# D weights copied by DMA into small float32r tiles and transposed from there

## Chip, cores and metric

The kernel runs on one core of one Trainium2 chip. The metric is the device time of one execution in microseconds (us), as the median of several runs. The names of the engines in the profile: PE is TensorE (matmuls, and transposes, which are matmuls with an identity), DVE is VectorE, ACT is ScalarE, POOL is GpSimd, SP is SyncE, which issues nearly all DMA transfers.

## What is computed

Two layers of a transformer encoder over 2048 tokens of width 1024. Each layer has an RMS norm, an input projection whose columns feed four groups of attention heads (A dense, B sliding window, C two-dimensional neighbourhood, D differential), a gate on every branch, an output projection and a residual add. The change touches group D, whose weights are a difference of two softmaxes:

```
def body(qi):                      # one block of 128 queries
    sc = einsum('bqkgcd,bskcd->cbkgqs', qi, k) * scale
    p = softmax(sc, axis=-1)       # c = 0, 1
    w = p[0] - lam * p[1]
    return einsum('bkgqs,bskd->bqkgd', w, v)
```

There are two key/value heads (kv), two query heads for each (g), and two halves c.

## The kernel before

**Stages of a layer.** First the D columns of the input projection are computed for all 16 token tiles. Then comes the *D stretch*: 32 D units (2 kv times 16 query tiles t), with the remaining projections (groups A, B and C) as *filler*. Then the pools of that part are closed (`switch`) and the units of A, B and C follow. The output projection ends the layer.

**A D unit.** `d_scores` loads the queries and the gate and makes, for each g and each c, four score matmuls S of 128x512 (line 496). VectorE copies each out of PSUM with its row maximum (line 497). After four of them a small step on VectorE (line 503, with the junk tile jk) makes the negative maximum, and ScalarE takes the exponential of the 128x2048 row in place (line 504). When both c of a g are done, `comb` (line 723) forms w on VectorE in the tile P, which holds both g: 128 x 2 x 2048 float32. Then `dense_front` runs in 8 slots: in each, four 128x128 float32 transposes go to one PSUM tile PTp (line 513), and one copy on ScalarE (line 474) puts the result back over the 256 columns of P that were read. After the eighth slot `dense_back` makes the outputs: O (line 520), 32 matmul instructions, and `fin_d` normalises, gates and stores.

**The order.** `drive` interleaves slots: while unit k is transposed, the scores of unit k + 1 are made, and `fillers` advances the projections by 12.2 steps a slot. The projection matmuls are called z (lines 320, 322, 324: three for each of 8 weight tiles). A scheduler then fixes the order on each engine at build time. It may move instructions of the D stretch forward and back, z above all. At run time every engine works its list strictly in order, SyncE too: a transfer whose wait is not met holds everything behind it on SyncE. In the A, B and C part the order on TensorE is that in which the code is written.

**Two ways to transpose.** `transpose_raw` (line 94) takes a float32r source and views PSUM as float32r. The other way, `PE.transpose` with `idn`, takes float32. `dense_front` uses the second.

**Other tiles of the change.** `gt` holds the gate of a unit, `st2` the staging tiles of the weights of the projections (wst) on their way from memory, 128 KB each.

```
for h in range(2):
    for a in range(2):
        j = i * 2 + a
        PE.transpose(tp[:, (h * 2 + a) * 128:(h * 2 + a + 1) * 128], p[:, h, j * 128:(j + 1) * 128], idn)
evac(p[:, :, c], tp.rearrange("p (h k) -> p h k", h=2), i in u["ev"])
```

Of the kernel before, what the change touches and what calls it, by code (L numbers as in the profile page):

```python
# [12 lines left out]
F32 = mybir.dt.float32  # L13
F32R = mybir.dt.float32r
# [9 lines left out]
NT = S // 128  # L24
# [3 lines left out]
GAP2 = 2  # L28
# [45 lines left out]
def trunk_kernel(ctx, tc, x, norm_g, w_in, w_out, qn_a, kn_a, sink_b, rpb_c, lam_q1, lam_k1, lam_q2, lam_k2,  # L74
                 subln_d, final_g, rope, bmask, out, depth=DEPTH):
    nc = tc.nc
# [15 lines left out]
    def transpose_raw(dst, src):  # L92

        PE.transpose(dst.bitcast(F32R), src, idr)
# [164 lines left out]
    for l in range(depth):  # L259
# [93 lines left out]
        with tc.tile_pool(name="wd", bufs=16, reuse_waits="tile") as wp, tc.tile_pool(name="st", bufs=3, reuse_waits="tile") as st:  # L353
# [13 lines left out]
            p1 = ExitStack()  # L367
# [71 lines left out]
            for t in range(NT):  # L439
                h = hs.pop(t)  # L440
# [21 lines left out]
        with tc.tile_pool(name="sm", bufs=6, reuse_waits="tile") as sm, \  # L462
# [7 lines left out]
            def evac(dst, src, on_v):  # L470
                if on_v:
                    V.tensor_copy(dst, src)
                else:
                    A.copy(dst, src)  # L474
# [4 lines left out]
            def tick():  # L479
                for e in list(later):  # L480
                    e[0] -= 1
                    if e[0] <= 0:
                        later.remove(e)
                        e[1]()
# [5 lines left out]
            def dense_scores(q_list, k_ap, scale, nscale, zacc, p):  # L490
                mx = sm.tile([128, 4], F32, tag="mx", name="mx")
                for j in range(4):
                    s = sps.tile([128, 512], F32, tag="s", name="S")
                    c = j * 512
                    for i, q in enumerate(q_list):
                        PE.matmul(s, lhsT=q, rhs=k_ap[:, c:c + 512], start=(i == 0), stop=(i == len(q_list) - 1))  # L496
                    V.tensor_scalar(p[:, c:c + 512], s, 1.0, None, op0=ALU.mult, op1=ALU.max, accum_out=mx[:, j:j + 1])  # L497
                    tick()
                    if j < 3:
                        yield  # L500
                nm = sm.tile([128, 1], F32, tag="nm", name="nm")
                jk = sm.tile([128, 4], F32, tag="jk", name="jk")
                V.tensor_scalar(jk, mx, nscale, None, op0=ALU.mult, op1=ALU.min, accum_out=nm)  # L503
                A.activation(p, p, ACTF.Exp, bias=nm, scale=scale, accum_out=zacc)  # L504


            def dense_front(u, i):
                p, c = u["p"], slice(i * 256, (i + 1) * 256)
                tp = next(tpool).tile([128, 512], F32, tag="t", name="PTp")
                for h in range(2):  # L510
                    for a in range(2):
                        j = i * 2 + a
                        PE.transpose(tp[:, (h * 2 + a) * 128:(h * 2 + a + 1) * 128], p[:, h, j * 128:(j + 1) * 128], idn)  # L513
                evac(p[:, :, c], tp.rearrange("p (h k) -> p h k", h=2), i in u["ev"])
# [91 lines left out]
                return rz  # L606

            def load_gate(g, t, i):
                gt = ov.tile([128, 128], F32, tag="gt", name="gt", bufs=7)
                if g == "C":  # L610
                    rg, ch = divmod(t, 2)
                    src = bass.AP(tensor=gc_d.tensor, offset=gc_d.offset + (256 * rg + 32 * ch) * 256 + i * 128,
                                  ap=[[16384, 4], [256, 32], [1, 128]])
                    nc.sync.dma_start(out=gt, in_=src)
                else:
                    nc.sync.dma_start(out=gt, in_=(gd_d[t] if g == "D" else gs_d[g, t])[:, i, :])
                return gt
# [108 lines left out]

            if True:
                ph2 = ExitStack()
                st = ph2.enter_context(tc.tile_pool(name="st2", bufs=5, reuse_waits="tile"))
                wp = ph2.enter_context(tc.tile_pool(name="w2", bufs=10, reuse_waits="tile"))  # L730
                zp = ph2.enter_context(tc.tile_pool(name="z2", bufs=2, reuse_waits="tile"))
                zps = ph2.enter_context(tc.tile_pool(name="zps2", bufs=2, space=PSUM, reuse_waits="tile"))
# [129 lines left out]
                def filler():  # L862
                    need = []
                    for c, tiles in plan:
                        need += [(c, t) for t in tiles]
                    last_use = {}
                    resident = {t: ht[l, t] for t in range(HALF)}
                    pend = pend_all
                    group = {}
                    for i, (c, tiles) in enumerate(plan):  # L870
                        group[i] = tiles
                    wcur = wpre + [load_w(wp, st, k, plan[0][0][1], 256) for k in range(len(wpre), KD)]
                    for i, ((grp, c0, post), tiles) in enumerate(plan):
                        nxt = plan[i + 1] if i + 1 < len(plan) else None
                        wnext = []
                        if i == 6:
                            build_rep(l, zp.tile([128, 256], F32, tag="qs", name="rbuf", bufs=3))
                        for n, t in enumerate(tiles):
                            lastt = n == len(tiles) - 1
                            if t not in resident:  # L880
                                h = big.tile([128, 2, D], F32R, tag="b", name="ht2")
                                nc.sync.dma_start(out=h.bitcast(F32), in_=ht_d[l, t])
                                resident[t] = h
                            h = resident[t]
                            z = zps.tile([128, 256], F32, tag="z", name="z")
                            for k in range(KD):
                                for _ in in_proj_k(z, h, wcur[k], k):
                                    yield
                                if k == KQ and len(pend) > 1:
                                    pend.pop(0)()  # L890
                                if k == 2 and i >= KA0:
                                    next(side, None)
                                if lastt and nxt and len(wnext) < KD:
                                    wnext.append(load_w(wp, st, len(wnext), nxt[0][1], 256))
                                yield
                            pend.append(post(grp, t, z) or (lambda: None))
                            if nxt and t not in nxt[1]:
                                resident.pop(t)
                                m = nxt[1][n] if len(nxt[1]) == len(tiles) else None
                                if m is not None and m not in resident:  # L900
                                    h = big.tile([128, 2, D], F32R, tag="b", name="ht2")
                                    nc.sync.dma_start(out=h.bitcast(F32), in_=ht_d[l, m])
                                    resident[m] = h
                            progress[0] += 1
                        wcur = wnext

                progress = [0]
                fill = filler()
                p1p = ph2.enter_context(tc.tile_pool(name="p1", bufs=1, reuse_waits="tile"))
                if True:  # L910
                    kds = {(0, 0): kd0[0], (0, 1): kd0[1]}

                    def get_kd(kv):
                        def f(c):
                            if (kv, c) not in kds:
                                k_ = big2.tile([128, S], F32R, tag="b", name="kdt")
                                nc.sync.dma_start(out=k_.bitcast(F32), in_=kd_d[0][:, c, :])
                                kds[kv, c] = k_
                            return kds[kv, c]
                        return f  # L920
                    units = [dict(kv=kv, t=t, k=get_kd(kv), qp=dv, s=d_scores, par=True, ns=16, nv=8, ev=(), fin=fin_d, fb=6 + kv,
                                  p1=p1p, fixed=False, gap=GAP2, front=dense_front, back=dense_back, get_o=own_o,
                                  v=lambda h, j, kv=kv: vd[:, j, kv * 64:(kv + 1) * 64]) for kv in range(2) for t in range(NT)]

                    for u in units:
                        u["fp"] = lambda: tps.tile([128, 512], F32, tag="t", name="fin")
                    for u in units[-2:]:
                        u["f1"], u["f2"] = 3, 5
                    units_d = [[u] for u in units]
# [64 lines left out]
            def b_scores(u):  # L994
                kv, t = u["kv"], u["t"]
                qh, qlo = u["q"]()
                u["g"] = load_gate("B", t, kv)
                j0, j1 = max(t - 1, 0), min(t + 2, NT)
                n = (j1 - j0) * 128
# [223 lines left out]
```

## Time and profile before

| | us |
|---|---|
| median of 3 runs | 3578.99 (3578.23 to 3581.57) |
| the profiled execution | 3577.38 |
| its span | 3575.6 |
| D stretch, layer 0: first S to last S | 184.2 to 1066.6 |
| D stretch, layer 1 | 1953.7 to 2834.6 |
| first S of group A | 1073.9 and 2841.8 |
| first matmul of the output projection | 1623 and 3390 |

The mean granted clock of TensorE is 0.99 of full speed. A row of a group names a line, an engine, an operation, the tiles (out<-in), shapes and a count, then the busy time, the mean duration in ns and the idle time ahead with what ended it. A row of a timeline begins with start and duration in us. Matmuls overlap each other, so their cost is read from the distance between starts. A row of windows begins with the stretch and its length, then busy us (and count) of PE, its weight loads PEld, DVE, ACT and POOL, then the granted clock, the busy share of the DMA engines and GB/s.

### The profile page before, as it was taken

How to read it: one execution, taken by the hardware profiler on the slowest of the kernel's cores; microseconds unless marked ns; L12 is line 12 of the kernel's file. 1: busy time of each engine (PE TensorE's matmuls, PEld its weight loads, DVE VectorE, ACT ScalarE, POOL GpSimd, SP SyncE). 2: the span in 40 equal slices, each digit the busy share in tenths (PEclk: the TensorE clock that was granted, in tenths of full speed). 3: DMA queues.
4: the chain of work that ended last, by engine and by line, in shares of the span. 5: the costliest groups of instructions: out<-in, count | busy, mean ns of one | idle time of the engine just before them, and what ended most of it. 6: DMA issues, size and time to landing. Idle time of an engine off the chain costs nothing.

```text
span 3575.6 us, 71573 instructions
## 1 busy us (share of the span) xinstructions
PE 3434.2 (96%) x25232; PEld 2961.5 (83%) x25232; DVE 2494.0 (70%) x7827; ACT 2110.5 (59%) x3963; POOL 955.3 (27%) x1604
## 2 busy tenths in 40 slices
PE   7999999999989999999999999999999899899999
PEld 7989889898967777887899898988889577688787
DVE  4377877778877887773233878787777788777733
ACT  4455656556667777771043556665566678777711
POOL 3455333553200001001034553256331000000000
PEclk9999999999999999999999999999999999999999
DMA  4532234333232345335435323253231332543243
GB/s 136 195 108 86 75 93 150 103 85 87 70 95 76 92 106 138 92 102 178 141 125 187 98 79 91 76 179 90 82 83 60 99 87 82 138 114 97 88 160 112
DMA packets 355777, 387.47 MB, mean 108 GB/s; under 512 B 59802, under 2 KB 298586, under 8 KB 350298
## 3 DMA queue, kind: packets, MB, share of 16 engines
q1 hardware_dynamic: 351098, 367.17, 34.7%
q10 hardware_dynamic: 4320, 15.73, 1.3%
q8 instruction: 199, 3.26, 0.4%
q14 instruction: 160, 1.31, 0.1%
HBM read 258.83 MB, written 123.91 MB: 107 GB/s over the span
## 4 chain that ended last, share of the span: by engine, by line
PE 78%; DVE 10%; DMA 3%; ACT 3%; POOL 2%; issue 2%; SPq 0%; DVEq 0%; ACTq 0%; POOLq 0%
PE O L520 11%; PE S L496 10%; PE y L218 10%; PE PTp L513 10%; PE z L320 10%; PE z L324 9%; PE z L322 9%; DVE P L497 4%; PE Obc L539 2%; PE PTp L531 2%; DVE P L723 2%; ACT P L504 2%; PE Sc L1043 1%; DVE wt L314 1%; DMA wst<-in_w_in_dram 1%
## 5 line engine op out<-in xcount | busy, mean ns | idle before, releaser
L497 DVE TENSOR_SCALAR_CACHE_REDUCE P<-S 128x512 f32<-128x512 f32 x1536 | 1025.4, 686 | 261.4 <-PE S L496 199.2
L320 PE MATMUL z<-wt,ht 128*128 128x256 f32 (+1 forms) x3008 | 890.5, 297 | 11.6 <-ACT wt L311 4.2
L322 PE MATMUL z<-wt,ht 128*128 128x256 f32 (+1 forms) x3008 | 885.1, 295 | 3.8 <-DVE wt L314 3.6
L324 PE MATMUL z<-wt,ht 128*128 128x256 f32 (+1 forms) x3008 | 883.1, 294 | 0.0
L513 PE MATMUL PTp<-idr,P 128*128 128x128 f32 x4096 | 627.6, 276 | 53.8 <-ACT P L474 25.8
L474 ACT COPY P<-PTp 128x512 f32<-128x512 f32 x896 | 511.8, 586 | 220.8 <-PE PTp L513 216.5
L513 PEld LDWEIGHTS PTp<-idr,P 128*128 128x128 f32 x4096 | 488.4, 142 | 158.1 <-ACT P L474 42.6
L504 ACT ACTIVATE P<-P,nm 128x2048 f32<-128x2048 f32 x256 | 513.9, 2008 | 171.3 <-DVE jk L503 164.1
L320 PEld LDWEIGHTS z<-wt,ht 128*128 128x128 f32 x3008 | 568.8, 189 | 30.8 <-POOL wt L313 4.7
L322 PEld LDWEIGHTS z<-wt,ht 128*128 128x128 f32 x3008 | 569.8, 190 | 18.3 <-DVE wt L314 6.4
L324 PEld LDWEIGHTS z<-wt,ht 128*128 128x128 f32 x3008 | 569.6, 189 | 8.1 <-issue 1.2
L496 PE MATMUL S<-kA,q 128*128 128x512 f32 x1024 | 361.0, 436 | 0.1
L218 PE MATMUL y<-wot,ms 128*128 128x512 f32 x1440 | 330.9, 392 | 0.0
L218 PEld LDWEIGHTS y<-wot,ms 128*128 128x128 f32 x1440 | 270.8, 188 | 59.7
L544 POOL TENSOR_TENSOR gg<-gt,rzh 128x128 f32<-128x128 f32 x192 | 76.9, 401 | 886.0 <-DVE rzh L605 324.5
L723 DVE SCALAR_TENSOR_TENSOR P<-P,cf,P 128x2048 f32<-128x2048 f32 x128 | 306.6, 2395 | 2.7
L504 ACT ACTIVATE P<-P,nm,rr_a 128x2048 f32<-128x2048 f32 x128 | 268.7, 2099 | 65.2 <-DVE jk L503 62.6
L313 POOL TENSOR_SCALAR wt<-wst,g 128x256 fp32r<-128x256 f32 (+1 forms) x336 | 211.6, 642 | 347.3 <-PE z L324 247.4
L520 PE MATMUL O<-P,vd 128*64 128x256 f32 x2048 | 238.5, 384 | 4.0 <-ACT P L474 3.9
L520 PE MATMUL O<-P,vA 128*64 128x256 f32 x2048 | 236.3, 384 | 0.0
L496 PE MATMUL S<-kdt,qd 128*128 128x512 f32 x512 | 215.3, 440 | 8.1 <-DVE P L497 5.4
L314 DVE SCALAR_TENSOR_TENSOR wt<-wst,g,wt 128x256 fp32r<-128x256 f32 (+1 forms) x344 | 194.6, 595 | 33.4 <-POOL wt L313 29.8
(195 smaller groups left out, 5125.9 us busy)
## 6 DMA issues: line engine op xcount, KB each, us to landing
wst<-in_w_in_dram SPq DMA_DIRECT2D x320, 128.0 KB
qd<-qd SPq DMA_DIRECT2D x128, 128.0 KB
htd<-ht SPq DMA_DIRECT2D x16, 1024.0 KB
ht<-htd SPq DMA_DIRECT2D x16, 1024.0 KB
q<-qsA SPq DMA_DIRECT2D x128, 128.0 KB
q<-qsB SPq DMA_DIRECT2D x64, 256.0 KB
q<-qc SPq DMA_DIRECT2D x64, 256.0 KB
mload<-mx ACTq DMA_DIRECT2D x30, 512.0 KB
```

The source lines that it names most:

```text
L218: PE.matmul(ys[c], lhsT=ms[:, a, kc], rhs=wts[k][:, b, c * 512:(c + 1) * 512], start=(k == 0 and i == 0), stop=(k == KD - 1 and i == 2))
L314: V.scalar_tensor_tensor(wt[:, 1, :], s, g8[:, k:k + 1], wt[:, 0, :].bitcast(F32), op0=ALU.mult, op1=ALU.subtract)
L320: PE.matmul(z, lhsT=h[:, 0, kc], rhs=wk[:, 0, :], start=(k == 0), stop=False)
L322: PE.matmul(z, lhsT=h[:, 0, kc], rhs=wk[:, 1, :], start=False, stop=False)
L324: PE.matmul(z, lhsT=h[:, 1, kc], rhs=wk[:, 0, :], start=False, stop=(k == KD - 1))
L474: A.copy(dst, src)
L496: PE.matmul(s, lhsT=q, rhs=k_ap[:, c:c + 512], start=(i == 0), stop=(i == len(q_list) - 1))
L497: V.tensor_scalar(p[:, c:c + 512], s, 1.0, None, op0=ALU.mult, op1=ALU.max, accum_out=mx[:, j:j + 1])
L504: A.activation(p, p, ACTF.Exp, bias=nm, scale=scale, accum_out=zacc)
L513: PE.transpose(tp[:, (h * 2 + a) * 128:(h * 2 + a + 1) * 128], p[:, h, j * 128:(j + 1) * 128], idn)
L520: PE.matmul(u["o"][a * 64:(a + 1) * 64, 0:256], lhsT=u["v"](0, j), rhs=u["p"][:, :, j * 128:(j + 1) * 128], start=(n < 2), stop=(n >= NT - 2))
L723: V.scalar_tensor_tensor(p0, p1, cf, p0, op0=ALU.mult, op1=ALU.add)
```

## The change

Per slot of a D unit, the 256 columns of P of both g (128 x 2 x 256 float32, 256 KB) are copied by a DMA on SyncE into a tile Pw of a new pool `stg` with two buffers. Pw is declared float32r, so the four transposes read it through `transpose_raw`. The copy back over P is unchanged. The last D unit of each layer keeps the old way. The gate tiles go from 7 to 6 buffers, the weight stages from 5 to 4, and jk from 6 to 4. TensorE thereby reads the D weights as float32r in these transposes.

```
-                jk = sm.tile([128, 4], F32, tag="jk", name="jk")
+                jk = sm.tile([128, 4], F32, tag="jk", name="jk", bufs=4)
...
                 tp = next(tpool).tile([128, 512], F32, tag="t", name="PTp")
+                if "stg" in u and u["t"] + u["kv"] * NT < 2 * NT - 1:
+                    w = u["stg"].tile([128, 2, 256], F32R, tag="sg", name="Pw")
+                    nc.sync.dma_start(out=w.bitcast(F32), in_=p[:, :, c])
+                    for h in range(2):
+                        for a in range(2):
+                            transpose_raw(tp[:, (h * 2 + a) * 128:(h * 2 + a + 1) * 128], w[:, h, a * 128:(a + 1) * 128])
+                    evac(p[:, :, c], tp.rearrange("p (h k) -> p h k", h=2), i in u["ev"])
+                    return
...
-                gt = ov.tile([128, 128], F32, tag="gt", name="gt", bufs=7)
+                gt = ov.tile([128, 128], F32, tag="gt", name="gt", bufs=6)
...
-                st = ph2.enter_context(tc.tile_pool(name="st2", bufs=5, reuse_waits="tile"))
+                st = ph2.enter_context(tc.tile_pool(name="st2", bufs=4, reuse_waits="tile"))
...
+                stg = ph2.enter_context(tc.tile_pool(name="stg", bufs=2, reuse_waits="tile"))
...
-                                  p1=p1p, fixed=False, gap=GAP2, front=dense_front, back=dense_back, get_o=own_o,
+                                  p1=p1p, stg=stg, fixed=False, gap=GAP2, front=dense_front, back=dense_back, get_o=own_o,
```

The scheduler orders the D stretch anew. On TensorE in layer 0, the end of the filler before the change: the last rows with z, then S, the transposes PTp and the first small matmul fin of a unit's normalisation.

```order
L322 MATMUL z<-wt,ht_8530 128x256
L324 MATMUL z<-wt,ht_8530 128x256
L496 MATMUL S<-kdt,qd 128x512
L590 MATMUL fin<-bones,sq 128x2
L513 MATMUL PTp<-idr,P 128x128 x4
L496 MATMUL S<-kdt,qd 128x512 x3
L513 MATMUL PTp<-idr,P 128x128 x4
L496 MATMUL S<-kdt,qd 128x512 x3
```

The same place now, again from the last two z on:

```order
L322 MATMUL z<-wt,ht_8773 128x256
L324 MATMUL z<-wt,ht_8773 128x256
L496 MATMUL S<-kdt,qd 128x512 x2
L94 MATMUL PTp<-idr,Pw 128x128 x4
L496 MATMUL S<-kdt,qd 128x512 x2
L557 MATMUL fin<-idr,gg 128x128
L496 MATMUL S<-kdt,qd 128x512 x2
L94 MATMUL PTp<-idr,Pw 128x128 x12
L496 MATMUL S<-kdt,qd 128x512
L94 MATMUL PTp<-idr,Pw 128x128 x4
```

Counted from the last z of layer 0 to the first S of group A, 43 S of D units stood there before and 71 stand there now: the last z has moved nearly two units ahead.

Behind the last z, on TensorE, one unit before, from its first S after the outputs O of the unit ahead to the last of its transposes:

```order
L496 MATMUL S<-kdt,qd 128x512
L513 MATMUL PTp<-idr,P 128x128 x2
L496 MATMUL S<-kdt,qd 128x512 x3
L590 MATMUL fin<-bones,sq 128x2
L513 MATMUL PTp<-idr,P 128x128 x4
L496 MATMUL S<-kdt,qd 128x512 x3
L513 MATMUL PTp<-idr,P 128x128 x8
L496 MATMUL S<-kdt,qd 128x512 x6
L549 MATMUL fin<-idr,gg 128x128
L513 MATMUL PTp<-idr,P 128x128 x16
```

And one unit there now:

```order
L496 MATMUL S<-kdt,qd 128x512 x4
L94 MATMUL PTp<-idr,Pw 128x128 x4
L496 MATMUL S<-kdt,qd 128x512 x2
L598 MATMUL fin<-bones,sq 128x2
L94 MATMUL PTp<-idr,Pw 128x128 x4
L496 MATMUL S<-kdt,qd 128x512 x2
L94 MATMUL PTp<-idr,Pw 128x128 x4
L496 MATMUL S<-kdt,qd 128x512 x2
L94 MATMUL PTp<-idr,Pw 128x128 x4
L496 MATMUL S<-kdt,qd 128x512 x4
L557 MATMUL fin<-idr,gg 128x128
L94 MATMUL PTp<-idr,Pw 128x128 x16
```

The transposes of the first slots stand further apart, with two S between; those of the last four slots still stand in one run, though each now reads a copy whose buffer is freed by the block two ahead of it.

On SyncE, a piece of the D stretch of layer 0 as it is now; before, there were no rows of Pw in it. The names: gsB stores a gate, wst loads weights, ht loads a stored 1 MB activation tile, gt loads a gate, mx stores a unit's result; what a row waits for stands behind it, DMAHW meaning an earlier transfer.

```order
L512 DMA Pw<-P 128x2x256 [waits DMAHW3_49,PE_49]
L804 DMA gsB_7_205<-gs 128x256 [waits DMAHW4_49,DVE_49]
L307 DMA wst<-in_w_in_dram 128x256 [waits DMAHW7_49,DVE_49]
L307 DMA wst<-in_w_in_dram 128x256 [waits DMAHW6_49,DMAHW0_49,DVE_49]
L307 DMA wst<-in_w_in_dram 128x256 [waits DMAHW1_49,DVE_49]
L512 DMA Pw<-P 128x2x256 [waits PE_49]
L512 DMA Pw<-P 128x2x256 [waits DMAHW3_49,PE_49]
L910 DMA ht_8304<-htd_9_1336 128x2048 [waits DMAHW2_49,PE_49]
L910 DMA ht_8367<-htd_10_1455 128x2048 [waits PE_49]
L624 DMA gt<-gd_0_120 128x128 [waits DMAHW4_49,Pool_49]
L512 DMA Pw<-P 128x2x256 [waits DMAHW5_49,DMAHW0_49,PE_49]
L561 DMA mx_10_234<-mix 128x128 [waits DMAHW6_49,DVE_49]
```

The copies of P stand in the same list as the loads and stores, 248 more of them per layer, and each keeps its place in it.

## The prediction

> **What bounds the kernel now.** I read the page's busy line first, then the chain that ended last, then the windows of the part that the change touches, and last the timeline of TensorE and the transfers that stand in the chain.
>
> ```profile
> span 3575.6 us, 71573 instructions
> PE 3434.2 (96%) x25232; PEld 2961.5 (83%) x25232; DVE 2494.0 (70%) x7827; ACT 2110.5 (59%) x3963; POOL 955.3 (27%) x1604
> PE 78%; DVE 10%; DMA 3%; ACT 3%; POOL 2%; issue 2%; SPq 0%; DVEq 0%; ACTq 0%; POOLq 0%
> ```
>
> TensorE is busy nearly throughout and carries 78% of the chain. But the mean hides two limits. I cut each layer's D stretch (first D score matmul S to the last) at the last projection matmul z. Column one after the window is its length, then busy us and counts by engine; the same windows follow for line 324 (a third of the z) and line 496 (the S) alone.
>
> ```profile
> 184.10:1016.00 831.90, 811.02 (x6303) 729.04 (x6302) 652.15 (x1969) 493.51 (x855) 341.56 (x570) 0.99 0.32 94
> 1016.00:1067.00 51.00, 39.02 (x210) 22.95 (x210) 43.97 (x145) 36.55 (x53) 5.79 (x8) 1.00 0.43 114
> 1953.60:2783.60 830.00, 807.60 (x6302) 727.70 (x6301) 650.85 (x1968) 493.20 (x855) 342.71 (x569) 0.99 0.32 94
> 2783.60:2835.00 51.40, 40.91 (x209) 26.80 (x207) 44.17 (x147) 36.21 (x53) 5.78 (x8) 0.87 0.40 113
> ```
>
> ```profile
> 184.10:1016.00 831.90, 365.53 (x1280) 243.33 (x1280) 0.99 0.32 94
> ```
>
> ```profile
> 184.10:1016.00 831.90, 188.84 (x470) 86.18 (x470) 0.99 0.32 94
> 1016.00:1067.00 51.00, 20.19 (x43) 7.77 (x43) 1.00 0.43 114
> ```
>
> While z is left (832 us), TensorE is busy 811: it is the bound, z filling every gap. Once z has run out (51 us), TensorE has 39 and VectorE 44, and the chain there runs on VectorE:
>
> ```profile
> 1030.56 2.35 DVE P L723
> 1032.91 1.83 DVE P L497 x6
> 1048.30 2.10 ACT P L504 x2
> 1050.95 2.35 DVE P L723
> ```
>
> One D unit (16 S, 8 slots) lasts 1050.95 - 1030.56 = 20.4 us there. So a cheaper transpose is worth its full price in the first stretch and nothing in the second, and z that is used up sooner lengthens the second.
>
> **The transposes.** The change turns 62 x 8 = 496 blocks of four (31 of the 32 D units of each layer) from float32 to float32r. The timeline has both kinds, and z:
>
> ```profile
> 608.67 0.60 PE L513 MATMUL PTp<-idr,P 128*128 128x128 f32 x4
> 609.03 0.48 PE L496 MATMUL S<-kd,qd 128*128 128x512 f32 x1
> 609.35 0.28 PE L320 MATMUL z<-wt,ht 128*128 128x256 f32 x1
> ...
> 1014.40 0.28 PE L320 MATMUL z<-wt,ht 128*128 128x256 f32 x1
> 1014.52 0.28 PE L322 MATMUL z<-wt,ht 128*128 128x256 f32 x1
> 1014.64 0.40 PE L496 MATMUL S<-kdt,qd 128*128 128x512 f32 x1
> ```
>
> ```profile
> 1192.29 0.46 PE L94 MATMUL kT<-idr,kl 128*128 128x128 f32 x4
> 1192.59 0.62 PE L513 MATMUL PTp<-idr,P 128*128 128x128 f32 x4
> ```
>
> ```profile
> 1876.61 0.84 PE L94 MATMUL xT<-idr,xt 128*128 128x128 f32 x8
> 1877.29 0.41 PE L320 MATMUL z<-wt,ht 128*128 128x384 f32 x1
> ```
>
> Starts are what counts, since ends are modelled. A float32 block holds TensorE from 608.67 to 609.35 less one S:
>
> ```profile
> 1014.80 0.25 PE S L496
> ```
>
> That is 0.68 - 0.25 = 0.43 us. The float32r block of four takes 1192.59 - 1192.29 = 0.30; in a run of eight a block takes 0.68 / 2 = 0.34, its weight loads no longer fetched ahead. The blocks will mostly stand alone between z, so I take 0.30: 0.13, rounded to 0.14 us saved a block (bounds 0.09 and 0.14), 0.07 per S at 8 blocks to 16 S.
>
> **The sum of one layer.** z starts 0.12 us apart (three rows make 3 x 1280 = 3840 of them): 3840 x 0.12 = 460.8. The other 831.9 - 460.8 = 371.1 us belong to 470 S with their transposes and O: 0.79 us per S. In the new order, 71 S stand behind the last z instead of 43 (counted over the whole stretch), so 441 stand before it. Ahead of the last z: 460.8 + 441 x (0.79 - 0.07) = 778.3. Behind it: 71 x 51.0 / 43 = 84.2. Together 862.5 against 882.9, 20.4 less; layer 1 by the same working (830.0 and 51.4) 20.2 less. Of 1.75 units' work moved past the last z, VectorE gives back most; that is why 496 x 0.14 = 69 us of transposes become 40.6.
>
> **The copies.** There is no copy of P in the trace of before. It is 256 KB in pieces of 1 KB; the nearest rows are the 256 KB transfers in the chain, from issue to landing, and one that had to queue:
>
> ```profile
> 1615.42 2.73 DMA wos<-in_w_out_dram
> 452.06 3.53 DMA qc<-qc
> 1347.50 9.12 DMA mx<-mix
> ```
>
> The Trainium skill ("DMA: Bandwidth & Descriptors", section "Anatomy of one DMA") gives about 2.0 us plus bytes / 436e3 on the software path, an estimate of 2.6 us for 256 KB; by it alone the copies would cost nothing in either stretch. This case's 2.73 for the same size nearly agrees. I take 3.1, between the first two rows; 2.7 and 3.5 are kept for the range, 9.1 for a rival.
>
> Two staging buffers mean that a copy can start only when the block two before has been transposed. *While z lasts*, 3840 z over 441 / 2 = 220 blocks is 17.4 z or 2.1 us a block, with two S 2.6 us: two blocks are 5.2 us, which cover 3.1. What breaks the cover is the queue: SyncE issues in order, and eight loads of 1 MB a layer and the waits of other transfers stand between copies.
>
> ```profile
> ht<-htd SPq DMA_DIRECT2D x16, 1024.0 KB
> ```
>
> ```profile
> SPq L796 <- DVE gs L348: 60.6, 27, 7.0
> SPq L616 <- POOL gg L544: 55.9, 21, 10.6
> SPq L307 <- DVE wt L314: 40.9, 59, 6.2
> ```
>
> These are us in total, times and longest of SyncE's waits in layer 0's D stretch. If each of the eight loads makes the next copy 0.75 us late beyond its cover, that is 6 us a layer (bounds: 0, and 17 at 2.1 us each: a load that takes 4.2 us at the 250 GB/s of a crowded window, the last number of the row below, less the 2.1 us of spare cover).
>
> ```profile
> 1016.00:1026.00 10.00, 7.48 (x43) 4.94 (x42) 9.53 (x35) 9.57 (x14) 3.59 (x4) 1.00 0.92 250
> ```
>
> *Behind the last z* the cover is gone. The new chain of a unit: four rounds of landing and block, 4 x (3.1 + 0.36) = 13.8, the eighth copy 0.5 later, one S and its maximum 1.0, the exponential 2.1, small steps 0.5, the combination 2.35: 20.3 us. That ties with VectorE's 20.4; at 3.5 it is 21.9, at 2.7 it is 18.7 and hidden. Two equal chains that wait for each other lose something: I take 1.0 us a unit, 71 / 16 = 4.4 units, 4.4 us a layer (0 to 7). SyncE's issue of a copy, by the row of a 256 KB load in small pieces (min/median/max ns), only delays what stands behind it:
>
> ```profile
> L948 SPq DMA_DIRECT2D kl<-ksC x16: 552/555/567, 1192.8 to 3078.5; - x16
> ```
>
> **The smaller edits.** The junk tile of line 503 (6 to 4 buffers) is written on VectorE alone and read by nobody: nothing. The gates' 7 to 6 buffers and the weight stage's 5 to 4 make loads start later that are needed a unit or eight projections later; nothing while that lead holds, 0 to 4 us if it does not. In the tail TensorE will also wait longer. The granted clock in layer 1's tail was already 0.87 against layer 0's 1.00, and the two tails took 51.4 and 51.0 us: price 0. The Trainium skill ("TensorE: Matmul & The Clock Gate", section "Part 1: The HAM clock gate") states that an idle window of about 3.4 us halves the clock, which speaks against copies that TensorE waits for; the 0.4 us between the tails is all that it costs here.
>
> **Total.** -40.6 + 2 x 6 + 2 x 4.4 = -19.8 us. The profiled execution took 3577.4 (span 3575.6 and 1.8 around it), which gives 3557.6; the runs' median 3579.0 stands 1.6 above it, so I forecast 3559.
>
> **The rivals.**
> - *Copies late on the queue (slower).* A copy per unit stands behind a SyncE wait and lands 1.0 us past its cover; TensorE executes in order, so S, z and O behind it wait too. 2 x 27.6 units x 1.0 = 55 in place of the 12: 3579 - 40.6 + 8.8 + 55 = 3602. For it: waits of 2.2 us on average for the gate stores (60.6 / 27) on the queue that the copies now share, and the 9.12 us row. Against: most of those waits belong to transfers that were simply early. It decides from 0.58 us a unit, where (40.6 - 8.8) / 55.2 is used up.
> - *Break-even.* Blocks save only 0.09 (2 x 220 x 0.05 = 22 us less), or landings of 3.5 us put 6.6 us a layer on the tail and 12 on the middle: 3576 to 3581, within 0.2%.
> - *All cover holds (faster still).* No late copy and a tail still paced by VectorE: 3579 - 40.6 = 3538. For it: 5.2 us of cover against 3.1; against: the shared queue.
>
> **How the numbers follow.** Forecast 0.50 (its own range 3547 to 3570, from the bounds of its two waits), all cover holds 0.10, break-even 0.18, late copies 0.22. About 0.2%, or 7 us, is what a measurement of this kernel can tell from no change. So faster is 0.60, same 0.18, slower 0.22. The range goes from 3535 (the third rival and a little) to 3597, which leaves out the upper half of the first rival.
>
> **What would show it.** Right: the float32r blocks of P 0.30 to 0.34 us apart from what follows, the last z of layer 0 near 184 + 778 = 962 us, 71 S behind it, TensorE's wait for the copies below 10 us a layer while z lasts, landing near 3 us, a tail unit of 20 to 22 us. Wrong: waits for the copy of tens of us ahead of the last z (first rival); a tail unit over 23 us; or a first stretch that shrinks less than the transposes do, which would mean that z was not the only thing that filled TensorE.

## The result and the profile after

The changed kernel takes 3658.4 us (median, 3656.5 to 3661.3) against 3580.3 for the kernel before in the same runs: a ratio of 1.0221, 95% interval 1.0209 to 1.0233. It is 78 us slower, where 20 us faster was forecast. All of it is lost in the two D stretches, which take 929.2 and 921.5 us instead of 882.4 and 880.9; from the first S of group A to the first y, layer 0 takes 546 us instead of 549.

The page of the changed kernel: TensorE's busy time rose by 13 us although its transposes became cheaper, and the copies' group shows the new wait (busy us and mean ns of one, then the idle time ahead).

```profile
span 3658.0 us, 73257 instructions
PE 3447.1 (94%) x25232; PEld 2942.0 (80%) x25232; DVE 2491.8 (68%) x7827; ACT 2114.6 (58%) x3963; POOL 946.4 (26%) x1604
L94 PE MATMUL PTp<-idr,Pw 128*128 128x128 f32 x1984 | 244.3, 249 | 73.3 <-DMA Pw<-P 54.9
```

The windows of both D stretches, cut at the last z, then line 496 (the S) alone:

```profile
184.10:1012.00 827.90, 783.90 (x6147) 700.94 (x6146) 618.28 (x1875) 472.61 (x821) 335.71 (x568) 0.98 0.53 160
1012.00:1113.40 101.40, 75.86 (x363) 45.85 (x361) 76.59 (x240) 59.07 (x87) 6.94 (x10) 0.72 0.52 160
1996.50:2816.50 820.00, 777.38 (x6147) 696.95 (x6147) 618.23 (x1875) 472.22 (x821) 337.50 (x567) 0.98 0.53 161
2816.50:2918.00 101.50, 72.87 (x362) 44.83 (x361) 76.73 (x240) 59.03 (x87) 6.93 (x10) 0.76 0.53 160
```

```profile
184.10:1012.00 827.90, 176.47 (x441) 80.30 (x441) 0.98 0.53 160
1012.00:1113.40 101.40, 34.88 (x71) 14.91 (x71) 0.72 0.52 160
```

The order is as forecast: 441 S ahead of the last z, 71 behind. The times are not. Ahead of the last z the forecast was 784 us and the trace has 828; TensorE's idle time there doubled from 21 to 44 us. Behind it the forecast was 88.6 and the trace has 101.4. The DMA share rose from 0.32 to 0.53.

What ends last behind the last z shows in the chain of waits of that part of layer 1, before and after. Before, VectorE and ScalarE carry it; now a third of it is copies on their way.

```profile
by line: DVE P L497 35.9%; DVE P L723 22.8%; ACT P L504 20.2%; issue 4.2%; PE PTp L513 1.9%; ACT P L474 1.7%; DVE jk L503 1.6%; DVE rz L719 1.5%; DVE rz L720 1.4%; POOL drs L114 1.4%; DVE cf L722 1.3%; DVE os L571 1.2%; PE fin L590 1.1%; PE
```

```profile
by line: DMA Pw<-P 32.8%; PE PTp L94 12.9%; DVE P L497 10.0%; PE S L496 9.5%; ACT P L504 8.5%; DVE P L731 7.0%; issue 6.1%; PE O L528 4.8%; ACT P L474 1.2%; SPq L561 1.2%; DVE jk L503 0.9%; PE fin L598 0.8%; DVE rz L727 0.7%; DVE rz L728 0.
```

One round of it, from the same chain (start, us, what): the combination ends, a copy flies for 2.48 us, its block runs, the next copy flies.

```profile
2898.27 2.35 DVE P L731
2900.62 0.03 DVE P L497
2900.65 2.48 DMA Pw<-P
2903.13 0.14 issue
2903.27 0.72 PE PTp L94 x4
...
2906.08 2.45 DMA Pw<-P
2908.53 0.04 issue
2908.57 0.75 PE PTp L94 x4
```

### The profile page after: what moved, and what is told of

Read it like the earlier page. It is cut to its first block, busy times and chain, and to the rows that moved or that the text cites. A ratio compares the mean times of both kernels' runs of the same rounds, so it can differ in the third digit from the quotient of the medians.

```text
span 3658.0 us, 73257 instructions
## 1 busy us (share of the span) xinstructions
PE 3447.1 (94%) x25232; PEld 2942.0 (80%) x25232; DVE 2491.8 (68%) x7827; ACT 2114.6 (58%) x3963; POOL 946.4 (26%) x1604
## 4 chain that ended last, share of the span: by engine, by line
PE 41%; DVE 4%; DMA 4%; issue 2%; POOL 2%; ACT 2%; SPq 0%; ACTq 0%; POOLq 0%; DVEq 0%
PE y L218 10%; PE O L528 5%; PE S L496 5%; PE z L320 5%; PE z L322 4%; PE z L324 4%; PE PTp L521 3%; PE PTp L94 2%; DMA Pw<-P 2%; DVE P L497 1%; PE Obc L547 1%; PE PTp L539 1%; ACT P L504 1%; PE Sc L1052 1%; DMA wst<-in_w_in_dram 1%
## 5 line engine op out<-in xcount | busy, mean ns | idle before, releaser
L320 PE MATMUL z<-wt,ht 128*128 128x256 f32 (+1 forms) x3008 | 893.8, 299 | 32.5 <-DVE qc L827 12.7
L313 POOL TENSOR_SCALAR wt<-wst,g 128x256 fp32r<-128x256 f32 (+1 forms) x336 | 203.8, 616 | 568.8 <-PE z L324 402.4
L521 PE MATMUL PTp<-idr,P 128*128 128x128 f32 x2112 | 322.9, 275 | 26.6 <-DVE P L472 12.5
L521 PEld LDWEIGHTS PTp<-idr,P 128*128 128x128 f32 x2112 | 252.3, 140 | 106.7 <-ACT P L474 24.2
L94 PE MATMUL PTp<-idr,Pw 128*128 128x128 f32 x1984 | 244.3, 249 | 73.3 <-DMA Pw<-P 54.9
L94 PEld LDWEIGHTS PTp<-idr,Pw 128*128 128x128 f32 x1984 | 217.0, 146 | 108.8 <-issue 40.1
L528 PE MATMUL O<-P,vd 128*64 128x256 f32 x2048 | 253.0, 403 | 4.3 <-ACT P L474 4.3
```

The costliest lines, as they stand in the source:

```text
L320: PE.matmul(z, lhsT=h[:, 0, kc], rhs=wk[:, 0, :], start=(k == 0), stop=False)
L528: PE.matmul(u["o"][a * 64:(a + 1) * 64, 0:256], lhsT=u["v"](0, j), rhs=u["p"][:, :, j * 128:(j + 1) * 128], start=(n < 2), stop=(n >= NT - 2))
```

## The experiments

The theory, once the result was known, was that waits for the copies and their traffic eat a gain that was itself forecast too large. Its rivals were the place of the copies in SyncE's list, the smaller edits, and VectorE as the bound. Ratios are against the kernel before, in the same runs.

Every edit makes the scheduler order the D stretch anew, so each run also differs in how many S stand behind the last z. Counted in the traces, both layers together:

| kernel | S behind the last z |
|---|---|
| before | 86 |
| e1_sizes | 68 |
| e2_direct, e12_direct_all_buffers | 90, 104 |
| e6_traffic, e13_small_traffic | 52, 78 |
| e7_extra_transpose, e11_three_transposes | 58, 58 |
| e8_half_combination | 46 |
| the changed kernel, e3_copy_f32, e4_no_tail | 142 |
| e5_pool_queue | 180 |
| e10_weights9, e9_ring3 | 145, 73 |

Without copies an S takes about 1.2 us behind the last z (51.0 / 43) and 0.78 us ahead of it (in e1_sizes, each z taken at 0.12 us). One S more behind the last z then costs some 0.42 us. This is an estimate, and it is used below where two runs differ in their order.

**The smaller edits alone.** The buffer counts of the change, no copies, float32 transposes:

```diff
-                if "stg" in u and u["t"] + u["kv"] * NT < 2 * NT - 1:
-                    w = u["stg"].tile([128, 2, 256], F32R, tag="sg", name="Pw")
-                    nc.sync.dma_start(out=w.bitcast(F32), in_=p[:, :, c])
...
-                    return
```

> No copies, float32 transposes as before; only the buffer counts of the change (gates 6, weight stages 4, junk tile 4) and the unused staging pool stay. Theory W (TensorE waits for copies that land late) and theory S (float32r saves less than the sum said): 3575 to 3583 us, as before. Rival O (smaller pools make loads late): over 3600 us.

Measured: 3571.5 us, ratio 0.9976 (0.9967 to 0.9985); the same kernel again, as a control for a later run (e14_small_copy_ring2), 3571.5 us, ratio 0.9969 (0.9958 to 0.9981).

> e1_sizes again on the same chip, so that e13_small_traffic is compared with it directly: 3569 to 3576.

So the smaller edits are worth about -9 us, not 0. They also reorder the program: 68 S stand behind the last z instead of 86, which by the estimate above is some 7 of the 9 us. Which of the three edits it is was not tried.

**Float32r without copies.** P's producers write float32r (the scores of one half are so rounded before the exponential), and the transposes read P itself:

```diff
-                    w = u["stg"].tile([128, 2, 256], F32R, tag="sg", name="Pw")
-                    nc.sync.dma_start(out=w.bitcast(F32), in_=p[:, :, c])
...
-                            transpose_raw(tp[:, (h * 2 + a) * 128:(h * 2 + a + 1) * 128], w[:, h, a * 128:(a + 1) * 128])
+                            transpose_raw(tp[:, (h * 2 + a) * 128:(h * 2 + a + 1) * 128], u["pr"][:, h, j * 128:(j + 1) * 128])
...
-                u["p"] = pp.tile([128, 2, S], F32, tag="p", name="P")
+                u["pr"] = pp.tile([128, 2, S], F32R, tag="p", name="P")
+                u["p"] = u["pr"].bitcast(F32)
```

> No copies: every writer of P writes it as float32r, so that the float32r transposes read P itself. The scores of one half are thereby rounded to float32r ahead of their exponential, which the reference does not do. W: the saving comes through, 3535 to 3545 us (3579 less some 40). S: 3565 us or more, because the blocks do not save 0.14 us or z does not fill what they free.

Measured: 3563.5 us, ratio 0.9949 (0.9934 to 0.9963). It beats both kernels, and puts the price of everything that comes with the copies at 3658 - 3563 = 95 us. But it is only 8 us under e1_sizes: float32r without copies brings far less than 40.6. Its windows of layer 0:

```profile
182.80:1008.70 825.90, 796.81 (x6298) 709.94 (x6297) 650.45 (x1962) 492.01 (x854) 338.69 (x570) 0.99 0.34 95
1008.70:1063.00 54.30, 44.35 (x214) 27.48 (x213) 46.11 (x153) 36.98 (x54) 5.86 (x8) 0.76 0.36 93
```

The same with all buffer counts of before:

> The kernel before with its own buffer counts, no staging and no copies: P is written as float32r by its producers and transposed from there (one half's scores are rounded to float32r before the exponential, as in e2_direct). e2_direct was 17 us under the kernel before, of which e1_sizes, the buffer counts alone, had 9. If the two add up, this gives 8 to 9 us less than before: 3567 to 3575. If the buffer counts do nothing by themselves, it is e2_direct's 3563.

Measured: 3571.8 us, ratio 0.9971 (0.9960 to 0.9983). The two effects add up: some -8 to -10 us for float32r, -8 to -9 for the buffer counts.

**Copies with float32 transposes.** The staging tiles are float32 and the transposes too:

> The copies stay as in the change, but Pw is float32 and the transposes are float32 as before. W: the copies alone cost what separates the change from its sum, 3658 - 3538 = 120 us, of which a busier TensorE can hide a part: 3670 to 3700 us. S: float32r was worth little, so this stands near the change, 3650 to 3668 us.

Measured: 3704.5 us, ratio 1.0343 (1.0324 to 1.0362). With copies float32r is worth 46 us, five times as much as without, and the float32 kernel stands just above the 3670 to 3700 of theory W. The number of S behind the last z is the same in both. TensorE stands 86 us at the copies with float32 blocks and 78 with float32r (counted as in the section on the prediction), so a longer block that delays the next copy makes at most some 8 us of the 46; most of the rest is the blocks themselves (36 us, worked out there). Why TensorE's time counts nearly in full here is not shown.

**No copies behind the last z.** The test ends six units earlier in each layer:

```diff
-                if "stg" in u and u["t"] + u["kv"] * NT < 2 * NT - 1:
+                if "stg" in u and u["t"] + u["kv"] * NT < 2 * NT - 6:
```

> Units 0 to 25 of each layer are copied and transposed as in the change, units 26 to 31 as before. The stretch behind the last z of layer 0 took 101 us in the changed kernel, and 71/43 of the old one would be 84. If the copies cost in both stretches: 3658 - 2 x 17 = 3624 us. If all the loss lies behind the last z: below 3585 us. If all lies ahead of it: 3650 us or more.

Measured: 3639.7 us, ratio 1.0161 (1.0146 to 1.0176), 19 us under the changed kernel. As many S stand behind the last z in both, so this is a like comparison: the tails take 88.9 and 87.9 us instead of 101.3 and 101.5 (last z to last S). The tail units of layer 1 are back at 19.8 to 20.6 us, and TensorE's wait for the copies halves. But with the copies of 26 of 32 units left, 76 of the 95 us remain, so most of the loss does not come from the copies behind the last z. The row has us in total, times, and the longest:

```profile
PE PTp L94 <- DMA Pw<-P: 26.5, 36, 2.4
```

**Another engine issues.** `nc.gpsimd.dma_start` in place of `nc.sync.dma_start`, the same copies:

> The change with the copies issued by GpSimd instead of SyncE. If the copies are late because they stand behind other transfers' waits in SyncE's list (theory Q), TensorE's waits for them shrink: 3600 to 3640 us. If they are late because two buffers leave one landing time between one block and the next but one (theory R), nothing is gained, and a longer landing on that queue costs: 3650 us or more.

Measured: 3785.1 us, ratio 1.0579 (1.0558 to 1.0599). Out of SyncE's list TensorE waits longer still for the copies, 92.4 us:

```profile
PE PTp L94 <- DMA Pw<-P: 92.4, 71, 3.8
```

That SyncE's list is the cause is not supported. But the copies now stand in GpSimd's list, among its own work, and 180 S instead of 142 stand behind the last z, so this run alone does not exclude it. The Trainium skill ("DMA: Bandwidth & Descriptors", section "Issuing engines are not separate DMA queues") says that all issuing engines share the same 16 DMA engines, so moving a transfer wins issue time and no bandwidth; this run shows no gain of either kind.

**The traffic alone.** Float32 transposes of P; behind each copy back SyncE copies the block to a staging tile that nobody reads:

```diff
                 evac(p[:, :, c], tp.rearrange("p (h k) -> p h k", h=2), i in u["ev"])
+                if "stg" in u and u["t"] + u["kv"] * NT < 2 * NT - 1:
+                    w = u["stg"].tile([128, 2, 256], F32R, tag="sg", name="Pw")
+                    nc.sync.dma_start(out=w.bitcast(F32), in_=p[:, :, c])
```

> Float32 transposes of P as before, with the change's buffer counts; the same 496 copies of 256 KB are issued on SyncE after the copy back over P, into the two staging buffers, and nobody reads them. Theories Q and R: nobody waits for a copy, so the time is that of the run with the buffer counts alone, 3571 to 3580 us. If the transfers themselves slow the others (theory T: rings, SyncE's issue time): 3600 us or more.

Measured: 3606.5 us, ratio 1.0076 (1.0061 to 1.0092), 35 us over e1_sizes. Then the same list with a sixteenth of the bytes (`w[0:8]` from `p[0:8, :, c]`):

> The kernel of e6_traffic (float32 transposes, 496 copies issued by SyncE behind each copy back, read by nobody), but each copy moves 8 partitions, 16 KB, instead of 128, 256 KB. SyncE issues as many transfers and waits at the same places. Theory B: the 35 us that e6_traffic stood over e1_sizes are the bytes, which slow the other transfers (the 1 MB loads landed in 7.6 us instead of 5.7): within 10 us of e1_sizes, 3565 to 3582. Rival Q: they are the list, since SyncE issues in order and stands at each copy until its block has been copied back, with the loads of the projection behind it: 25 to 40 us over e1_sizes, 3596 to 3612, and the 1 MB loads land as in e1_sizes.

Measured: 3569.9 us, ratio 0.9971 (0.9961 to 0.9980), beside 3571.5 for e1_sizes on the same chip. As many entries in SyncE's list, each behind its block's copy back, cost nothing; the bytes cost the 35 us. Layer 0's D stretch of e6_traffic, then of e13_small_traffic (DMA share and GB/s at the end):

```profile
184.10:1078.20 894.10, 848.57 (x6508) 750.64 (x6506) 690.97 (x2112) 527.38 (x908) 338.67 (x578) 0.98 0.55 165
```

```profile
183.20:1062.80 879.60, 846.46 (x6508) 747.82 (x6506) 692.52 (x2112) 527.60 (x908) 337.52 (x578) 0.99 0.37 100
```

The busy times agree within 0.4%; of the 14.5 us between the two, 12.4 are idle time of TensorE (45.5 against 33.1). From issue to landing, the 16 loads of 1 MB took a median of 7.6 us with the traffic and 5.8 with the small copies (worked out from the traces' landing times). The order hides a part of the difference rather than making it, since e6_traffic has fewer S behind the last z (52 against 78). Which waits the 35 us come out of was not followed further.

**A fifth transpose.** e1_sizes with one float32 transpose more in each of the 496 blocks:

> No copies, the change's buffer counts, and a fifth float32 transpose in each of the 496 blocks, a repetition of the fourth. It is the price of TensorE's time in the D stretch. If the first stretch is TensorE's as the prediction had it, 440 of the 496 count at 0.109 us: 3571 + 48 = 3619 us. If a unit's chain through VectorE and ScalarE sets much of it (theory C): 3571 to 3595 us.

Measured: 3603.4 us, ratio 1.0066 (1.0051 to 1.0081). A transpose costs 0.110 us between z (z to z over a block: 0.584 us instead of 0.475, medians), 496 of them 54.6 us; the time rose by 32, or 59% of it.

**Three transposes.** One fewer; the copy back reads the second block for the fourth, so that part of P is not transposed:

> The kernel of e1_sizes (no copies, float32 transposes) with three float32 transposes in each of the 496 blocks instead of four; the copy back reads the second for the fourth, so the output is not the reference's. 54 us of TensorE's time go, the mirror of e7_extra_transpose, where 54 us more cost 32. Theory V: TensorE is not the only bound of the stretch before the last z; in units with few z the chain over VectorE and ScalarE sets the length, and cheaper blocks only let z run out sooner, so the gain is far under 32: 5 to 18 us under e1_sizes' 3571.5. Rival F: the price of TensorE's time is the same both ways, and float32r blocks gained only 8 us in e2_direct because writing float32r costs elsewhere: 28 to 36 us under e1_sizes.

Measured: 3539.6 us, ratio 0.9887 (0.9872 to 0.9902), 32 us under e1_sizes. The price is 59% in this direction too, and the theory that units short of z give nothing back falls: a us of TensorE's time in these blocks is worth about 0.59 us of the kernel. Both runs have 10 S fewer behind the last z than e1_sizes, some 4 us by the estimate above, so the price lies between 0.51 and 0.66.

**Half the combination.** VectorE combines 1024 of each 2048 keys; the other half of P stays uncombined:

> No copies, the change's buffer counts, and the combination of the two softmax halves on VectorE done for 1024 of 2048 keys only, so half the weights lack their second term. It takes 1.2 us off VectorE 128 times. If TensorE sets the first stretch, only the 43 S behind the last z gain, 2 x 2.7 units x 2.4 = 13 us: 3555 to 3565 us. Theory C: 64 units x 2.4 = 154 us less VectorE work shows in part ahead of the last z too: 3530 us or less.

Measured: 3520.8 us, ratio 0.9831 (0.9815 to 0.9848), 51 us under e1_sizes. An instruction takes 1.32 us instead of 2.40, 128 of them 138 us less, so a us of VectorE is worth up to 0.37 (22 S fewer behind the last z are some 9 of the 51 us). Neither engine bounds the D stretch alone.

**Three staging buffers.** `bufs=3` for the staging pool; one of the projection's ten weight buffers goes to make room, so the control has nine and two:

> The changed kernel with 9 weight buffers for the projection instead of 10 and nothing else, the control for e9_ring3. Weights are needed eight at a time, so a buffer less leaves one of lead instead of two: 0 to 15 us above the changed kernel's 3658.

Measured: 3675.0 us, ratio 1.0263 (1.0248 to 1.0279), some 15 us over the changed kernel by the ratios, at the upper end of the range.

> The changed kernel with three staging buffers instead of two; the projection's weight buffers go from 10 to 9 to make room, as in e10_weights9, with which this run is compared. Theory R: a block waits because its copy may start only when the block two before has been read, so each block has to hide a landing of 2.6 us in one block's work where few z are left; three buffers give it two blocks' work, and most of the some 78 us that TensorE stands at the copies' blocks go: 30 to 55 us under e10_weights9, the unit times behind the last z fall from 21 to 24 us to near 20.5. Rival T: the copies cost by what they take from other transfers and from SyncE's list, 35 us in e6_traffic, which a third buffer leaves as it is: within 10 us of e10_weights9.

Measured: 3621.0 us, ratio 1.0102 (1.0082 to 1.0122): 54 us under the control. TensorE's wait for the copies, control first, then three buffers:

```profile
L94 PE MATMUL PTp<-idr,Pw 128*128 128x128 f32 x1984 | 245.5, 249 | 69.2 <-DMA Pw<-P 54.3
```

```profile
L94 PE MATMUL PTp<-idr,Pw 128*128 128x128 f32 x1984 | 234.7, 247 | 45.5 <-DMA Pw<-P 30.8
```

The landing is as long in both (2.56 and 2.60 us, medians). But the program's order changed too: 73 S stand behind the last z instead of 145. The windows behind the last z in both layers, control first, then three buffers:

```profile
1006.20:1107.90 101.70, 72.82 (x355) 44.69 (x355) 75.20 (x235) 57.20 (x83) 6.93 (x10) 0.74 0.53 155
...
2825.70:2933.10 107.40, 77.40 (x376) 46.27 (x374) 81.19 (x260) 62.82 (x90) 9.61 (x12) 0.76 0.51 154
```

```profile
1030.60:1094.00 63.40, 46.15 (x210) 28.07 (x210) 46.04 (x150) 36.94 (x53) 7.40 (x8) 0.69 0.64 179
...
2835.60:2878.70 43.10, 30.98 (x165) 19.18 (x164) 31.97 (x102) 24.98 (x39) 4.75 (x6) 0.83 0.77 220
```

That is 209.1 us for 145 S and 106.5 for 73: 1.44 and 1.46 us each. Behind the last z an S is no faster with three buffers, against theory R's unit of 20.5 us (16 S at 1.46 are 23), and ahead of it TensorE stands 28 us at the copies in both kernels. The stretches are shorter because fewer S stand in the slow one: at 1.44 us an S there and 0.83 ahead, 72 S fewer make some 44 of the 55 us between the two traces' D stretches (an estimate). So this run does not show what the wait for a free buffer costs; it shows that the scheduler, given a third buffer, keeps z for longer.

## Why the prediction was wrong

Three steps of the sum failed: a block's saving (-40.6 us, where the same working with the measured 0.073 us gives -11), the waits for the copies (12 + 8.8 us, where TensorE stood 27 us ahead of the last z and the copies behind it cost 19 to 26), and the bytes (nothing, where they cost 35 us).

**The order and the landing: right.** 441 and 71 S as forecast; copies land in 2.56 us (median of the 496, worked out from the landing times), under the 3.1 taken. They did not need to be slow to be late.

**A block saves 0.14 us: wrong, it saves 0.07.** The rows show it, the changed kernel's first, for the same sequence as the prediction's 608.67 to 609.35:

```profile
595.95 0.46 PE L94 MATMUL PTp<-idr,Pw 128*128 128x128 f32 x4
596.25 0.47 PE L496 MATMUL S<-kd,qd 128*128 128x512 f32 x1
596.55 0.40 PE L320 MATMUL z<-wt,ht 128*128 128x256 f32 x2
```

The float32r block holds TensorE from 595.95 to 596.55 less the S of 0.25: 0.35 us against 0.43. Over 107 such blocks alone between z, start of the z ahead to the third z behind is 0.720 us, over 41 before 0.793: 0.073 saved. The 0.30 was taken from a block up to the next transpose; the 0.43 also held what the block delays in the matmul behind it. Like was not compared with like, and the bounds of 0.09 and 0.14 left the truth out. So 496 blocks give 36 us, not 69. In the prediction's working, with 0.0365 us less per S instead of 0.07, a layer takes 877.3 us instead of 882.9, and the two layers together gain 11 us, not 40.6.

**The price of TensorE's time: wrong.** The prediction took TensorE for the bound while z is left and counted a us saved there in full; by that e7_extra_transpose would have stood at 3619, and it stood at 3603. Without copies a us of TensorE's time in the blocks is worth about 0.59 us (e7, e11), and VectorE's time counts too (e8). That 40.6 of 69 us is also 59% is chance: there the rest goes to the S that moved behind the last z. At 59%, 36 us are worth 21. The direct kernels gained 8 and 10, and by the estimate above their order took back 9 and 8 (22 and 18 S more behind the last z than in e1_sizes and the kernel before), which closes most of the gap.

**5.2 us of cover hide 3.1: wrong.** The number was a mean over a stretch. Two buffers tie each copy to the block two before; and a unit's first copy can start only when the combination is done (2900.62 in the chain above). Where z are few or absent, the landings show. TensorE waited 54.9 us for copies by the page; taking each block's start less that of the instruction ahead, beyond 0.33 us, gives 78 us, 51 behind the last z and 27 ahead of it, against the 12 + 8.8 of the sum. What the copies behind the last z cost the kernel is less than the standing: 26 us between the tails of the changed kernel and e4_no_tail, 19 between their medians. The price of the 27 us ahead no run isolates.

**Queue loss from SyncE's list: a small part.** The first rival (3602) priced late copies at 55 us and put them down to SyncE's order. That the page's wait is 54.9 is chance. e13_small_traffic shows that as many entries behind the copies back cost nothing. In the changed kernel's own trace, the time from which a copy could start is the end of the block two before or of the combination, whichever is later; copies that SyncE issued later than that account for at most 22 of the 78 us, 14 of them ahead of the last z. Most of the rest is landing.

**Left out of the sum: the bytes.** 130 MB more, a DMA share of 0.53 instead of 0.32, hardly any change in the engines' busy times, and 35 us (e6_traffic). The sum knew a copy only as something that TensorE waits for.

**The tail tie.** The chain of 20.3 us was built as the trace has it, four rounds of copy and block. In layer 0 the last four units took 26.0, 22.8, 21.4 and 23.5 us, not 21.4. A block in the chain quoted above runs for 0.72 to 0.75 us, where the sum had 0.36; the granted clock from 2903.3 to 2909.3 is 0.50. And VectorE, which was to pace the tail, is idle there for 24.8 of 101.4 us, before for 7.0 of 51.0. The tail missed by 12.7 us in layer 0, the stretch ahead of the last z by 44 (layer 1: 12 and 38).

**Clock, price 0.** The granted clock of the tails fell to 0.72 and 0.76, and TensorE idles there for a quarter of the time. The Trainium skill's rule that idle windows halve the clock ("TensorE: Matmul & The Clock Gate", section "Part 1: The HAM clock gate") agrees in direction. The share of idle time alone does not decide it: before, TensorE idled for 12.0 of the 51.0 us of layer 0's tail, nearly a quarter too, at 1.00. The 0.4 us between two tails without copies was no measure of what the clock costs here, and no run isolates it.

**Smaller edits, 0:** they gave 9 us, some 7 of them by the order, which in the changed kernel is another one.

The sum again: 3580 - 11 (blocks and order, by the prediction's working) + 35 (bytes) + 27 (standing ahead of the last z) + 19 to 26 (copies behind it) = 3650 to 3657, where 3658 was measured. This is an estimate. It counts TensorE's time in full, for which e3_copy_f32 speaks and e7 and e11 do not; and the 35 us were measured with another order. That it comes out so near is partly luck.

## What to carry to other kernels

A copy's cover is the work between the moment when its buffer comes free and the moment when it is read, place by place: a mean over a stretch hides the places without any. Price added bytes on their own, beside the waits: here they cost 35 us, in a kernel that waits for none of them. Measure a cheaper matmul to the start of what follows it, on both sides in the same neighbourhood. And where a scheduler orders every kernel anew, compare the orders before a difference between two runs is put down to the edit.

## What the runs showed that was not expected

- The float32r block's gain of 0.13 us, as the prediction had it from two places of one trace, is 0.07 between other matmuls.
- 496 transfers of 16 KB more in SyncE's list cost nothing (3569.9 against 3571.5 us), 496 of 256 KB cost 35 us, and loads of 1 MB took 7.6 us instead of 5.8, at a mean of 165 GB/s in layer 0's D stretch.
- Fewer buffers made the kernel 9 us faster, twice.
- A third staging buffer gave 54 us although the time of an S behind the last z and TensorE's standing ahead of it stayed as they were: 73 S instead of 145 stood behind the last z.
